# When a hybrid encoder layer fetches its parked residual, parked half embedding, norm weights and embedding input

## Chip, cores and metric

One NeuronCore of one Trainium2 chip runs the whole layer in one launch. The metric is device time in microseconds (us) of one execution. Before the change the median of three runs is 1164.94 us (1162.43 to 1167.7).

## What is computed

One layer on 256 tokens of width 2048, all float32. The part that matters here is the second half:

```
h  = h + rms_norm(mixed, g_mix_post)
fn = rms_norm(h, g_ffn_pre)
ff = (silu(fn @ w_ffn_gate) * (fn @ w_ffn_up)) @ w_ffn_down      # 2048 -> 5632 -> 2048
h  = h + rms_norm(ff, g_ffn_post)
gate = sigmoid(rms_norm(h, g_ple_pre) @ w_ple_gate)
ple  = p @ w_ple_proj                                            # 256 -> 2048
h  = h + rms_norm(gate * ple, g_ple_post)
```

## The kernel before

Every product is made of three fp32r matmuls: a float32 operand is split into a high and a low part, and high x high, high x low and low x high are summed in PSUM (lines 661 to 663). The weights stream through SBUF in tiles of 512 KB (256 rows x 512 columns): SyncE (SP) issues the load of a raw tile `wr` (line 522), ScalarE (ACT) casts it to the high part `wh` (line 614), VectorE (DVE) subtracts to get the low part `wl` (line 627), and TensorE (PE) uses both in 12 matmuls of 128x512. There are 4 buffers of `wr` and 4 pairs of `wh` and `wl`. A raw buffer is free once its `wl` is made; a pair is free once PE has used it. So the load of a tile waits for the `wl` of the tile four before it, and the cast of a tile waits for the last matmul of the tile four before it.

The feed-forward part runs over the 5632 columns in three parts (`PARTS`). In each part the gate and up products of its column blocks come first, then the down products of that part. The last part's down products take 24 weight tiles, called D1 to D24 here: D1 to D12 for output columns 0 to 1023, D13 to D24 for the rest. The last tile ahead of D1 is the last tile of `w_ffn_up`, called U here. The activations of the last block pass DVE (lines 1714 and 333), are moved between partitions by 16 small transfers `mT` (line 343; 8 issued by SP, 8 by POOL), are split on ACT and DVE (`mid2h`, `mid2l`, lines 305 and 307), and are used by D9 to D12 and D21 to D24.

Four things that are too large to keep, or are needed only later, are fetched again near the end:

- the residual `h`, parked in DRAM at line 1589 and fetched by `reload_h` (line 1596) in two transfers of 1024 KB. It is used at line 1535, after the last down product.
- the first half of the embedding `ple`, parked at line 1608 and fetched by `reload_half` (line 1614, 1024 KB). It is used when the gate of the embedding is applied (line 1856).
- the norm weights `g_ffn_post`, spread over all partitions by `next_gain` and `load_gain` (line 1422, 1024 KB). They are used at line 1478, when an output block of the down products is complete.
- the embedding input `pT`, fetched by `load_pT` (line 1410, tile `pw`, 256 KB) and split on ACT and DVE (lines 305 and 307, `pTh` and `pTl`). The products of `w_ple_proj`, after D24, use it.

The order of instructions on each engine is made at build time by a planner (`Plan`): every helper is a generator that yields the engine and the estimated cost of its next instruction, and the planner emits the instruction that could start first. A task gets two numbers: the time from which it is ready (`ready`), and a bonus (`late`, negative is earlier). The planner holds a transfer to be landed a fixed 2 us after its estimated duration (`LATENCY`). On the chip the order is fixed: each engine takes its instructions in that order, and an instruction whose data is not there holds up what stands behind it on its engine.

Of the kernel before, what the change touches and what calls it, by code (L numbers as in the profile page):

```python
# [18 lines left out]
NT = S // P  # L19
# [50 lines left out]
SOON = 2.0  # L70
# [6 lines left out]
class Event:  # L77


    t = None  # L80
# [141 lines left out]
def dve(n, take=None, give=None):  # L222
    return ("dve", COST["dve"] + 0.00104 * n, None, take, give)
# [6 lines left out]
def dma(kb, take=None):  # L230
    return ("dma", kb / 340.0, None, take, None)
# [3 lines left out]
def layer(ctx: ExitStack, tc: tile.TileContext, a: dict, out: bass.AP):  # L235
    nc = tc.nc
# [4 lines left out]
    plan = Plan(wr=R_BUFS, w=W_BUFS, sm=SM_BUFS, acc=4, ev=1, mid=2, bt=2, m2=1, mt=1, sq=1, T0=1, T1=1, T4=1, **{f"{s}{j}": n for s, m, n in (("p", 3, 1), ("t", 3, 0)) for j in range(m)}, wr0=1, w0=1)  # L241

    def f32(t):
        return t.bitcast(F32)
# [14 lines left out]
    def w_kind(i):  # L259
        return f"w{more_w[i]}" if i in more_w else "w"  # L260
# [15 lines left out]
    def raw_kind(i):  # L276
        if i in lower:
            return f"p{lower[i]}"
        return f"wr{more_raws[i]}" if i in more_raws else "wr"
# [22 lines left out]
    def split(hi, lo, src, n, give=None):  # L302

        yield act(n)
        nc.scalar.copy(hi, src)
        yield dve(n, give=give)
        nc.vector.tensor_tensor(out=lo, in0=src, in1=f32(hi), op=ALU.subtract)
# [57 lines left out]
    def done(event):  # L365
        event.t = plan.now
# [63 lines left out]
    class Group:  # L430
# [23 lines left out]
        def two(self, j):  # L454
            i = len(tiles)
            tiles.append(None)
            self.twos.append(i)
            lower[self.own[j] + 1] = j
            segs.append((two_products, self, j, i))
# [47 lines left out]
    def pieces(i):  # L507

        return [slice(0, 1), slice(1, 2)] if i < EARLY else [slice(0, 2)]
# [77 lines left out]
    def last_sum(i):  # L587
        late, last, j, js, _, _ = fours[i]
        b = (3, 6, 7)[j]
        there = Event()  # L590
        yield from added(blocks()[:, b, :], late[:, 0, :], there)
        yield there
        if j == js[-1]:
            raws[last] = blocks()[:, 3:7:3, :] if len(js) == 2 else blocks()[:, 7:8, :]
            done(ev_raw[last, 2])
# [21 lines left out]
    def lo_stream():  # L617
        last_one = max(f[1] for f in fours.values())
        for i in range(len(tiles)):
            at_lo[0] = i  # L620
            for j in pieces(i):
                n = j.stop - j.start
                yield ev_hi[i, j.stop]
                src = raws[i] if n == 2 else raws[i][:, j, :]
                m = slice(j.start, j.start + src.shape[1])
                yield dve(src.shape[1] * N, give=gives.get(i) or raw_kind(i) if j.stop == 2 else None)
                nc.vector.tensor_tensor(  # L627
                    out=los[i][:, m, :], in0=src, in1=f32(his[i][:, m, :]), op=ALU.subtract
                )
                done(ev_lo[i, j.stop])  # L630
            raws.pop(i)
            if i == half_end:
                plan.add(reload_half(), plan.now, -SOON)
            if i in fours:
                plan.add(last_sum(i), plan.now, -2 * SOON)
            if i == last_one:
                done(ev_ple)
# [31 lines left out]
    def product(dst, x, i, j, start=False, stop=False, seeded=False):  # L669
        plan.main(3 * MM)  # L670
        wh, wl = his[i][:, j, :], los[i][:, j, :]
        nc.tensor.matmul(dst, x[0], wh, start=start, stop=False, skip_group_check=seeded)  # L672
        nc.tensor.matmul(dst, x[1], wh, start=False, stop=False, skip_group_check=seeded)  # L673
        nc.tensor.matmul(dst, x[0], wl, start=False, stop=stop, skip_group_check=seeded)  # L674

    def spent(i):
        his.pop(i), los.pop(i)
        at_pe[0] = max(at_pe[0], i)
        free_w(i)
        plan.run()  # L680

    def block(lhs, kx, t):
        return [x[:, t * P : (t + 1) * P] for x in lhs.at[kx]]
# [49 lines left out]
    def two_products(group, j, i):  # L733
        (C1, _, _), (C2, _, _) = group.chunks
        kx = group.sevens[j][1]
        s = group.lhs.sums[kx]
        plan.main(0, ev_lo[i, 2], group.lhs.ev[kx + 1], group.made)
        product(C1.accs[0], block(group.lhs, kx + 1, 0), i, 0, seeded=True)
        product(C2.accs[0], s["S4"], i, 1, seeded=True)
        spent(i)  # L740
        if i == last_two:
            plan.add(reload_h(), plan.clk["pe"], -SOON)
        if i == last_third:
            plan.add(load_pT(), plan.clk["pe"], -SOON)

    def one_product(group, js, i):
        (C1, _, _), _ = group.chunks
# [39 lines left out]
    def free_w(i):  # L787
        if i not in keep:
            plan.free[w_kind(i)].append(plan.clk["pe"])
        if i == max(more_w):  # L790
            plan.add(next_gain(("ffn", "g_ffn_post"), plan.clk["pe"]), plan.clk["pe"])

    keep = set()
    def run_seg(s):
# [580 lines left out]
    t2 = {}  # L1375
# [27 lines left out]
    def pT_pair():  # L1403
        return [t2["pool"].tile([P, 2, S], F32R, tag=n, name=n) for n in ("pTh", "pTl")]

    def load_pT():
        yield dma(256, take="mt")
        here = Event()
        pw = t2["pool"].tile([P, 2, S], F32, tag="mt", name="pw")
        nc.sync.dma_start(pw, a["pT"].rearrange("(k p) s -> p k s", p=P))  # L1410
        done(here)
        yield here
        hi, lo = pT_pair()
        yield from split(hi, lo, pw, 2 * S, give="mt")
        pT[1].blocks(hi, lo, 0, 2)
        pT[1].pair(0)
    ev_gain = {}

    def load_gain(n):
        yield dma(1024)  # L1420
        g = t2["pool"].tile([P, D], F32, tag="gain", name=f"gain_{n}")
        nc.sync.dma_start(g, a[n].to_broadcast([P, D]))
        t2["gain"] = g
# [136 lines left out]
    def turn_h(c, hi, lo, nxt, gname):  # L1560
# [18 lines left out]
    spill = ctx.enter_context(  # L1579
        tc.tile_pool(name="spill", bufs=1, space=bass.MemoryType.DRAM)  # L1580
    ).tile([NT, P, D], F32, name="h_spill")
    ev_spilled, ev_back = Event(), Event()
# [6 lines left out]
            nc.sync.dma_start(spill[t], t2["h"].tiles[t])  # L1589
        done(ev_spilled)  # L1590

    def reload_h():
        t2["h"] = Halves(t2["pool"], "h")
        for t in range(NT):
            yield dma(1024)
            nc.sync.dma_start(t2["h"].tiles[t], spill[t])
        done(ev_back)

    half_spill = ctx.enter_context(
        tc.tile_pool(name="half_spill", bufs=1, space=bass.MemoryType.DRAM)  # L1600
# [11 lines left out]
    def reload_half():  # L1612
        yield dma(1024)
        nc.sync.dma_start(t2["ple"][:, :, 0 : D // 2], half_spill)
        done(ev_half_back)

    def next_gain(g, ready):
        yield from load_gain(g[1])
        done(ev_gain[g[0]])
# [63 lines left out]
    ffn = Sub("ffn", "g_ffn_post", "g_ple_pre")  # L1683
# [332 lines left out]
    for i, (_, last, _, js, _, two) in fours.items():  # L2016
        ev_load[i], ev_load[i + 1] = Event(), Event()
        gives[i], gives[i + 1], gives[two] = f"T{first_slot[i]}", raw_kind(i), raw_kind(i + 1)
        gives[last] = tuple(f"t{j}" for j in js)
    twos = [(j, i) for f, g, j, i in (s for s in segs if s[0] is two_products)]  # L2020
    last_two = max(i for _, i in twos)
    last_third = max(i for j, i in twos if j == 2)
# [22 lines left out]
    plan.add(hi_stream(), late=lambda: lateness(at_hi))  # L2045
    plan.add(sum_stream(), late=-LATE)
    plan.add(lo_stream(), late=lambda: lateness(at_lo))
    plan.add(make_hT(0), late=lambda: -2 * LATE if at_hi[0] else -LATE)
    plan.add(make_hT(1), late=lambda: -2 * LATE if at_hi[0] else -LATE)
# [96 lines left out]
```

## Time and profile before

| | |
|---|---|
| runs | 1162.43, 1164.94, 1167.7 us |
| profiled execution | 1163.89 us, span 1162.1 us |
| TensorE busy | 1148.7 us of the span, mean granted clock 0.997 |
| DVE, ACT busy | 883.0 us, 703.0 us |
| DMA | 257.21 MB, mean 221 GB/s |
| D1 starts, D24 ends | 990.1 us, 1055.4 us after the span's start |

A row of a timeline gives the start and the duration in us, the engine (a q marks the issue of a transfer by the engine's sequencer), the line, the operation, output <- inputs, the shape and the number of instructions merged into the row; in square brackets is how long the engine had been idle and who ended that. A row of transfers gives their number, the KB of one, and the median us from issue to landing. A row of stretches gives for each engine its busy time and its number of instructions, then the granted clock, the busy share of the DMA engines and their GB/s.

### The profile page before, as it was taken

Reading aid. Unit: us, or ns where it says so; the run is one execution under the profiler, and the core shown is the slowest. Engines: PE = TensorE matmul, PEld = TensorE weight load, DVE = VectorE, ACT = ScalarE, POOL = GpSimd, SP = SyncE. Lnnn points to the kernel's source line nnn. Section 1 sums busy time; section 2 is a strip of 40 time slices with the busy share of each in tenths; the row PEclk is TensorE's granted clock in tenths of the full one; section 3 lists DMA queues with packets and bytes.
Section 4 is the critical chain, followed back from the end, with each engine's and each line's share of the span. In section 5 each row is a group of like instructions: output and inputs, shape, how many; then the busy total and the mean of one; then the engine's idle time right before and its main releaser. Section 6 shows DMA issues by size and latency. Waiting matters only on the chain.

```text
span 1162.1 us, 15025 instructions
## 1 busy us (share of the span) xinstructions
PE 1148.7 (99%) x5225; PEld 951.3 (82%) x5225; DVE 883.0 (76%) x1096; ACT 703.0 (60%) x933; POOL 120.9 (10%) x198
## 2 busy tenths in 40 slices
PE   9999999999999999999999999999999999999997
PEld 7888888888888888788888888888888887887786
DVE  6678787888468777988778888887778884668575
ACT  6777777875456655655546556565455554456564
POOL 0000000000000123031000223312000311100000
PEclk9999999999999999999999999999999999999999
DMA  9867566546676887876775777877667668854772
GB/s 315 288 188 222 185 181 206 175 149 211 228 272 197 291 256 226 261 215 203 252 224 190 249 224 205 263 239 216 207 208 252 205 216 291 249 190 161 216 248 77
DMA packets 109964, 257.21 MB, mean 221 GB/s; under 512 B 38976, under 2 KB 46144, under 8 KB 108736
## 3 DMA queue, kind: packets, MB, share of 16 engines
q1 hardware_dynamic: 99552, 241.73, 62.5%
q0 software_dynamic: 9904, 14.17, 7.4%
q8 instruction: 41, 0.67, 0.2%
q10 hardware_dynamic: 432, 0.35, 0.1%
q14 instruction: 35, 0.29, 0.1%
HBM read 242.57 MB, written 5.24 MB: 213 GB/s over the span
## 4 chain that ended last, share of the span: by engine, by line
PE 86%; DMA 5%; DVE 4%; ACT 2%; issue 1%; POOL 1%; SPq 0%; ACTq 0%; DVEq 0%; POOLq 0%
PE acc L663 23%; PE acc L662 23%; PE acc L661 23%; PE acc L674 4%; PE acc L673 4%; PE acc L672 4%; DMA mT<-mid 3%; DVE wl L627 1%; POOL mT L343 1%; PE tr L324 1%; ACT wh L614 1%; DMA wr<-in_w_ple_gate 1%; DMA pw<-in_pT 1%; PE warm L2055 0%; PE pg L355 0%
## 5 line engine op out<-in xcount | busy, mean ns | idle before, releaser
L627 DVE TENSOR_TENSOR wl<-wr,wh 128x1024 fp32r<-128x1024 f32 (+1 forms) x313 | 373.9, 1209 | 131.7 <-ACT wh L614 129.7
L614 ACT CAST wh<-wr 128x1024 fp32r<-128x1024 f32 (+1 forms) x313 | 323.8, 1043 | 212.0 <-PE acc L662 142.0
L661 PE MATMUL acc<-wh,hT_mix_hi 128*128 128x512 f32 x420 | 164.4, 391 | 2.6 <-ACT wh L614 2.6
L662 PE MATMUL acc<-wh,hT_mix_lo 128*128 128x512 f32 x420 | 164.1, 391 | 0.3 <-DVE hT_mix_lo L313 0.3
L663 PE MATMUL acc<-wl,hT_mix_hi 128*128 128x512 f32 x420 | 164.2, 391 | 0.1
L343 POOL DMA_DIRECT2D mT<-mid x152 | 88.5, 589 | 570.0 <-DMA wr<-in_w_ffn_up 401.9
L663 PE MATMUL acc<-wl,hT_hi 128*128 128x512 f32 x320 | 124.9, 391 | 0.0
L661 PE MATMUL acc<-wh,hT_hi 128*128 128x512 f32 x316 | 124.4, 394 | 0.0
L662 PE MATMUL acc<-wh,hT_lo 128*128 128x512 f32 x316 | 123.1, 390 | 0.0
L661 PEld LDWEIGHTS acc<-wh,hT_mix_hi 128*128 128x128 f32 x420 | 79.2, 189 | 19.3 <-ACT wh L614 3.0
L614 ACT CAST wh<-ple 128x1024 fp32r<-128x1024 f32 (+1 forms) x52 | 51.8, 995 | 70.6 <-DVE ple L566 26.5
L663 PEld LDWEIGHTS acc<-wl,hT_mix_hi 128*128 128x128 f32 x420 | 79.1, 188 | 17.5 <-DVE wl L627 1.3
L662 PEld LDWEIGHTS acc<-wh,hT_mix_lo 128*128 128x128 f32 x420 | 79.2, 189 | 17.3 <-DVE hT_mix_lo L313 1.0
L663 PEld LDWEIGHTS acc<-wl,hT_hi 128*128 128x128 f32 x320 | 60.1, 188 | 13.6 <-DVE wl L627 0.9
L627 DVE TENSOR_TENSOR wl<-ple,wh 128x1024 fp32r<-128x1024 f32 (+1 forms) x52 | 59.6, 1150 | 13.7 <-ACT wh L614 13.1
L662 PEld LDWEIGHTS acc<-wh,hT_lo 128*128 128x128 f32 x316 | 59.4, 188 | 11.7
L661 PEld LDWEIGHTS acc<-wh,hT_hi 128*128 128x128 f32 x316 | 59.4, 188 | 11.3
L583 POOL DMA_DIRECT2D ple<-in_w_ffn_up x27 | 24.0, 887 | 245.1 <-DVE wl L627 164.7
L627 DVE TENSOR_TENSOR w<-wr,w 128x1024 fp32r<-128x1024 f32 x29 | 35.4, 1220 | 10.3 <-ACT w L614 9.7
L614 ACT CAST w<-wr 128x1024 fp32r<-128x1024 f32 x29 | 30.5, 1052 | 19.7 <-PE acc L662 14.5
L627 DVE TENSOR_TENSOR wl<-third,wh 128x1024 fp32r<-128x1024 f32 x29 | 35.4, 1221 | 8.6 <-ACT wh L614 7.7
L661 PE MATMUL acc<-wh,hT_ffn_hi 128*128 128x512 f32 x104 | 40.9, 393 | 0.6 <-ACT hT_ffn_hi L311 0.6
(429 smaller groups left out, 2389.9 us busy)
## 6 DMA issues: line engine op xcount, KB each, us to landing
wr<-in_w_in SPq DMA_DIRECT2D x77, 512.0 KB, 4.6
wr<-in_w_ffn_gate SPq DMA_DIRECT2D x70, 512.0 KB, 5.3
wr<-in_w_ffn_down SPq DMA_DIRECT2D x70, 512.0 KB, 4.7
wr<-in_w_ffn_up SPq DMA_DIRECT2D x55, 512.0 KB, 5.7
wr<-in_w_out SPq DMA_DIRECT2D x32, 512.0 KB, 4.0
wr<-in_w_ple_gate SPq DMA_DIRECT2D x32, 512.0 KB, 4.5
lower<-in_w_ffn_up SPq DMA_DIRECT2D x18, 512.0 KB, 5.0
third<-in_w_ffn_gate SPq DMA_DIRECT2D x18, 512.0 KB, 5.9
```

Source lines behind the costliest of these rows:

```text
L324: nc.tensor.transpose(tr[:, b, t * P : (t + 1) * P], e[:, t, sl], ident)
L343: (nc.gpsimd if i in pool else nc.sync).dma_start(dst[32 * j : 32 * j + 32, :, :, i, :], src[32 * i : 32 * i + 32, :, :, j, :],)
L583: nc.gpsimd.dma_start(dst, src, accum_op=ALU.add)
L614: nc.scalar.copy(his[i][:, 0 : src.shape[1], :] if n == 2 else his[i][:, j, :], src)
L627: nc.vector.tensor_tensor(out=los[i][:, m, :], in0=src, in1=f32(his[i][:, m, :]), op=ALU.subtract)
L661: nc.tensor.matmul(accs[t], hi[:, sl], his[i][:, j, :], start=st, stop=False, **group)
L662: nc.tensor.matmul(accs[t], lo[:, sl], his[i][:, j, :], start=False, stop=False, **group)
L663: nc.tensor.matmul(accs[t], hi[:, sl], los[i][:, j, :], start=False, stop=sp, **group)
L672: nc.tensor.matmul(dst, x[0], wh, start=start, stop=False, skip_group_check=seeded)
L673: nc.tensor.matmul(dst, x[1], wh, start=False, stop=False, skip_group_check=seeded)
L674: nc.tensor.matmul(dst, x[0], wl, start=False, stop=stop, skip_group_check=seeded)
```

## The change

The times from which the four fetches are ready are moved, and the two halves of the residual become two tasks of their own. The bonus that had put them ahead of the weight tiles is gone.

```diff
@@ lo_stream
             if i == half_end:
-                plan.add(reload_half(), plan.now, -SOON)
+                plan.add(reload_half(), plan.now + 64.0)
@@ two_products
         if i == last_two:
-            plan.add(reload_h(), plan.clk["pe"], -SOON)
+            for t in range(NT):
+                plan.add(reload_h(t), plan.clk["pe"] + 28.0 + 13.0 * t)
         if i == last_third:
-            plan.add(load_pT(), plan.clk["pe"], -SOON)
+            plan.add(load_pT(), plan.clk["pe"] + 22.0)
@@ free_w
         if i == max(more_w):
-            plan.add(next_gain(("ffn", "g_ffn_post"), plan.clk["pe"]), plan.clk["pe"])
+            plan.add(next_gain(("ffn", "g_ffn_post"), plan.clk["pe"] + 27.0), plan.clk["pe"] + 27.0)
@@ reload_h
-    def reload_h():
-        t2["h"] = Halves(t2["pool"], "h")
-        for t in range(NT):
-            yield dma(1024)
-            nc.sync.dma_start(t2["h"].tiles[t], spill[t])
-        done(ev_back)
+    halves_back = []
+
+    def reload_h(t):
+        if "back" not in t2:
+            t2["back"] = Halves(t2["pool"], "h")
+        yield dma(1024)
+        nc.sync.dma_start(t2["back"].tiles[t], spill[t])
+        halves_back.append(t)
+        if len(halves_back) == NT:
+            t2["h"] = t2["back"]
+            done(ev_back)
```

On SP, the queue of transfers from the last two gate and up tiles to the end of the down tiles was this before the change (the rows of `w_ffn_down` are D1 to D24 in order):

```order
L1614 DMA ple<-ple_spill 128x2x1024
L1422 DMA gain_g_ffn_post<-in_g_ffn_post 128x2048
L1596 DMA h_8087<-h_spill 128x2048
L522 DMA wr<-in_w_ffn_gate 128x1024
L522 DMA wr<-in_w_ffn_up 128x1024
L522 DMA wr<-in_w_ffn_down 128x1024
L1596 DMA h_8088<-h_spill 128x2048
L522 DMA wr<-in_w_ffn_down 128x1024
L1410 DMA pw<-in_pT 128x2x256
L522 DMA wr<-in_w_ffn_down 128x1024 x4
L343 DMA mT<-mid 32x8x32 x8
L522 DMA wr<-in_w_ffn_down 128x1024 x18
```

The same stretch of SP's queue with the change:

```order
L522 DMA wr<-in_w_ffn_gate 128x1024
L522 DMA wr<-in_w_ffn_up 128x1024
L522 DMA wr<-in_w_ffn_down 128x1024 x6
L343 DMA mT<-mid 32x8x32 x8
L522 DMA wr<-in_w_ffn_down 128x1024 x4
L1423 DMA gain_g_ffn_post<-in_g_ffn_post 128x2048
L1599 DMA h_8084<-h_spill 128x2048
L1411 DMA pw<-in_pT 128x2x256
L522 DMA wr<-in_w_ffn_down 128x1024 x4
L1599 DMA h_8085<-h_spill 128x2048
L522 DMA wr<-in_w_ffn_down 128x1024 x6
L1620 DMA ple<-ple_spill 128x2x1024
```

All five fetches have moved behind U. The norm weights, the first half of the residual and the embedding input now stand in a row between D10 and D11, the second half of the residual between D14 and D15, and the half embedding between D20 and D21.

On ACT, the casts before the change around the split of the embedding input (the one cast ahead of `pTh` is that of the last gate tile, the three behind it are those of U, D1 and D2):

```order
L305 CAST mid2h_7734<-mT 128x512 x2
L614 CAST wh<-wr 128x1024
L305 CAST pTh<-pw 128x512
L614 CAST wh<-wr 128x1024 x3
L1695 ACTIVATE mid<-acc_7774,rstd_f 128x512
L1695 ACTIVATE mid<-acc_7775,rstd_f 128x512
L614 CAST wh<-wr 128x1024 x4
L305 CAST mid2h_8304<-mT 128x512 x2
L614 CAST wh<-wr 128x1024 x9
L1496 ACTIVATE junk,ss_ffn<-mg 128x512 x2
```

The same stretch of ACT with the change:

```order
L305 CAST mid2h_7734<-mT 128x512 x2
L614 CAST wh<-wr 128x1024 x4
L1701 ACTIVATE mid<-acc_7774,rstd_f 128x512
L1701 ACTIVATE mid<-acc_7775,rstd_f 128x512
L614 CAST wh<-wr 128x1024 x4
L305 CAST mid2h_8293<-mT 128x512 x2
L614 CAST wh<-wr 128x1024 x3
L305 CAST pTh<-pw 128x512
L614 CAST wh<-wr 128x1024 x6
L1497 ACTIVATE junk,ss_ffn<-mg 128x512 x2
```

The split of the embedding input has moved from ahead of the cast of U to between the casts of D9 and D10. On DVE its second half (`pTl`) has moved in the same way, from ahead of the `wl` of U to between the `wl` of D9 and D10. Nothing else changes its place on ACT or DVE, and PE and POOL keep their order.

## Prediction

> **What bounds the kernel now.** The page comes first. It says which engine sets the time:
>
> ```profile
> span 1162.1 us, 15025 instructions
> PE 1148.7 (99%) x5225; PEld 951.3 (82%) x5225; DVE 883.0 (76%) x1096; ACT 703.0 (60%) x933; POOL 120.9 (10%) x198
> ```
>
> PE is busy for 99% of the span, so the kernel gets faster only where PE stands still or runs slowly. The fetches that move stood between 960 and 976 us, and the next view is the list of waits from 980 us to the end (who waited for whom, total, times, longest):
>
> ```profile
> ACT pTh L305 <- DMA pw<-in_pT: 5.9, 1, 5.9
> PE acc L661 <- ACT wh L614: 2.6, 1, 2.6
> ```
>
> ACT waited 5.9 us for the embedding input, and PE waited 2.6 us for a cast of ACT, each once. The timelines of PE and of ACT show that the two belong together:
>
> ```profile
> 982.56 0.39 PE L663 MATMUL acc<-wl,hT_mix_hi 128*128 128x512 f32 x1
> 985.53 0.80 PE L661 MATMUL acc<-wh,hT_mix_hi 128*128 128x512 f32 x1 [2.59 <-ACT wh L614]
> ...
> 990.13 0.39 PE L661 MATMUL acc<-wh,mid2h 128*128 128x512 f32 x1
> ```
>
> ```profile
> 977.00 1.05 ACT L614 CAST wh<-wr 128x1024 fp32r<-128x1024 f32 x1 [3.06 <-DMA wr<-in_w_ffn_gate]
> 983.92 0.62 ACT L305 CAST pTh<-pw 128x512 fp32r<-128x512 f32 x1 [5.87 <-DMA pw<-in_pT]
> 984.44 2.93 ACT L614 CAST wh<-wr 128x1024 fp32r<-128x1024 f32 x3
> ```
>
> The split `pTh`, which nothing needs before D24 is done, stood in ACT's queue ahead of the cast of U. Its data came at 983.9, so the cast of U began at 984.44, and PE's first matmul with U at 985.53 instead of 0.227 us after 982.56. It did not resume at full speed either. The stretches show why (columns: PE, PEld, DVE, ACT, POOL, granted clock, DMA share, GB/s):
>
> ```profile
> 984.00:986.00 2.00, 0.47 (x1) 0.47 (x2) 1.18 (x2) 2.00 (x3) 0.00 (x0) 0.86 0.05 20
> 986.00:988.00 2.00, 1.96 (x5) 1.06 (x5) 2.00 (x3) 2.00 (x4) 0.00 (x0) 0.50 0.18 31
> ```
>
> The granted clock fell to 0.50 behind the pause. So the price of the wait is read from start to start. D15 and D1 stand 14 tiles apart, and D10 is between them:
>
> ```profile
> 1014.61 0.39 PE L661 MATMUL acc<-wh,mid2h 128*128 128x512 f32 x1
> ...
> 1028.21 0.39 PE L661 MATMUL acc<-wh,mid2h 128*128 128x512 f32 x1
> ```
>
> (1028.21 - 990.13) / 14 = 2.72 us for one weight tile without a pause, 0.227 us for a matmul. U would have begun at 982.56 + 0.23 = 982.79 and D1 at 985.51. D1 began at 990.13, so the wait cost **4.62 us**: 2.74 of standing still, 1.88 at the low clock.
>
> **Step 1: the wait at U goes.** Why was `pw` late? SP's timeline, and behind it the transfers with their time to landing:
>
> ```profile
> 959.98 0.60 SPq L1614 DMA_DIRECT2D ple<-ple_spill  x1
> 963.26 0.33 SPq L1422 DMA_DIRECT2D gain_g_ffn_post<-in_g_ffn_post  x1
> 963.64 1.09 SPq L1596 DMA_DIRECT2D h<-h_spill  x1
> 968.09 0.33 SPq L522 DMA_DIRECT2D wr<-in_w_ffn_gate  x1
> 969.46 0.33 SPq L522 DMA_DIRECT2D wr<-in_w_ffn_up  x1
> ```
>
> ```profile
> ple<-ple_spill SPq DMA_DIRECT2D x1, 1024.0 KB, 9.8
> gain_g_ffn_post<-in_g_ffn_post SPq DMA_DIRECT2D x1, 1024.0 KB, 9.9
> h<-h_spill SPq DMA_DIRECT2D x1, 1024.0 KB, 12.0
> wr<-in_w_ffn_gate SPq DMA_DIRECT2D x1, 512.0 KB, 8.8
> pw<-in_pT SPq DMA_DIRECT2D x1, 256.0 KB, 7.9
> ```
>
> Landings follow the order of issue: 969.8, 973.2, 975.6 for the three of 1024 KB, 976.9 for the last gate tile. With the five fetches out of the way, the gate tile and U are issued at the same 968.09 and 969.46, since these times are set by `wl` of earlier tiles. They land after 3.4 to 4.6 us, the fastest and the median of this row of tile `wr` from 955 to 1060 us:
>
> ```profile
> DMA to landing us min/median/max: 3.4/4.6/8.8
> ```
>
> That is 974.1 at the latest for U. Its cast then needs only a free pair, which PE gives back when the tile four before U ends, at 982.79 - 3 x 2.72 = 974.6. What would be late next? Even with 8.8 us, U would be there at 978.3 and ready by 980.6, before 982.79, so no other wait stands close behind the removed one. Nothing is added or removed in work: the same transfers, casts and subtractions run, and one more task is none on the chip. Gain: 4.62 us, and everything behind moves up by that.
>
> **Step 2: `pTh` waits again, now ahead of the cast of D10.** By the order on SP, `pw` stands behind D7 to D10, the norm weights and one half of `h`. D7 is issued when the eight `mT` are, and these wait for a transpose on DVE that hangs on the end of U:
>
> ```profile
> 992.46 5.70 SPq L343 DMA_DIRECT2D mT<-mid  x8
> 998.26 38.36 SPq L522 DMA_DIRECT2D wr<-in_w_ffn_down  x18
> ```
>
> ```profile
> 1002.42 1.05 ACT L614 CAST wh<-wr 128x1024 fp32r<-128x1024 f32 x1 [0.60 <-DMA wr<-in_w_ffn_down]
> ...
> 1004.94 1.06 ACT L614 CAST wh<-wr 128x1024 fp32r<-128x1024 f32 x1 [0.21 <-DMA wr<-in_w_ffn_down]
> 1006.42 1.06 ACT L614 CAST wh<-wr 128x1024 fp32r<-128x1024 f32 x1 [0.42 <-PE acc L662]
> ```
>
> These casts are of D7, D9 and D10. D7 and D9 waited for their landing, at 1002.4 and 1004.9: 1.26 us for 512 KB. 4.62 us earlier D9 lands at 1000.3 and D10 at 1001.6. The norm weights, `h` and `pw` are 2304 KB, 4.5 times 512 KB, so 5.7 us: `pw` lands at 1007.3. The cast of D10 follows 0.52 us later at 1007.8. In the old rows `wl` of D10 began 1.09 us after its cast and took 1.22:
>
> ```profile
> 1007.51 1.22 DVE L627 TENSOR_TENSOR wl<-wr,wh 128x1024 fp32r<-128x1024 f32 x1 [0.26 <-ACT wh L614]
> ```
>
> so it is done at 1010.1. PE reaches D10 at 1014.61 - 4.62 = 1009.99 and needs `wl` at its third matmul, 0.45 us later, at 1010.44. The margin is 0.3 us, where it was 6.3. I take **0 us** here. Bounds: below, 0, since PE cannot gain at a place where it did not wait; above, the two transfers of 1024 KB landed 3.4 and 2.4 us behind their forerunners in the crowd at 960 us, which adds 0.7 to the three and makes the loss 0.4; at the 2.3 us that the rival below takes, it is 2.0.
>
> The Trainium skill (HBM Reference, "Specifications (TRN2)") gives about 358 GB/s as the effective rate of one core and calls more than that the case of a core that streams alone. By 358 GB/s, as an estimate from that page, the three transfers take 6.6 us and step 2 costs 0.6 us; the 1.26 us of this trace are 416 GB/s, and they decide.
>
> **Step 3: D15 comes later.** The load of D14 is issued when `wl` of D10 is done, at 1010.1 and no longer at 1008.76 - 4.62 = 1004.1. The second half of `h` stands behind D14, and D15 behind that. D14 lands 3.4 us (fastest) to 4.6 us (median) later, at 1013.5 to 1014.7; `h` adds 2.5, D15 1.3, so D15 lands at 1017.3 to 1018.5. Its old cast and what stands behind it on DVE:
>
> ```profile
> 1020.02 1.05 ACT L614 CAST wh<-wr 128x1024 fp32r<-128x1024 f32 x1 [1.67 <-PE acc L662]
> 1020.98 0.62 ACT L1496 ACTIVATE junk<-mg 128x512 f32<-128x512 f32 x1
> ```
>
> ```profile
> 1021.73 1.31 DVE L1478 TENSOR_TENSOR mg<-mg,gain_g_ffn_post 128x512 f32<-128x512 f32 x2 [0.79 <-ACT junk L1496]
> ...
> 1024.49 1.31 DVE L1478 TENSOR_TENSOR mg<-mg,gain_g_ffn_post 128x512 f32<-128x512 f32 x2 [0.26 <-ACT junk L1496]
> 1025.71 3.49 DVE L627 TENSOR_TENSOR wl<-wr,wh 128x1024 fp32r<-128x1024 f32 x3
> ```
>
> The squares (`junk`) wait behind the cast of D15, the products with the norm weights wait for the squares, and `wl` of D15 waits for those: one chain without slack. `wl` of D15 ended at 1025.71 + 1.22 = 1026.9, PE needed it at 1028.21 + 0.45: 1.7 us of margin. The cast moves from 1015.4 (the old one less 4.62) to 1017.3 or 1018.5, 1.9 to 3.1 us later, so PE waits 0.2 to 1.4 us. I take **0.5 us**, nearer to the fast landing because the queue is already running when D14 joins it.
>
> **What costs nothing.** The norm weights land at about 1004 and are used from about 1018. The second half of `h` is there by 1018 and needed after D24, about 1051. The half embedding puts 2.5 us ahead of D21. The load of D21 is issued when `wl` of D17 is made, which PE needs by 985.51 + 16 x 2.72 + 0.45 = 1029.5; from then the two take at most 2.5 + 4.6 us, the cast and `wl` 2.3, so D21 is ready at 1038.9, and PE needs it at 1040.4. If that cover went, each microsecond would be one of PE. The `mT` of the block before, which POOL issued while the five fetches ran, only get faster.
>
> **The sum.** 4.62 - 0 - 0.5 = 4.1 us off the profiled execution, 1163.89 to 1159.8 us. That execution lies 1.05 us under the median of the three runs; off the median the forecast is 1164.94 - 4.1 = **1160.8 us**.
>
> **Rivals.** *(a) The wait moves instead of going.* If `pw` lands later than 1007.6, ACT holds up D10 as it held up U, and each further microsecond is one of PE. For it: the same instruction, again ahead of a cast that PE needs soon, with 4096 KB in front of its transfer from D7 on. Against: the 1.26 us of the rows. If the three take 8 us instead of 5.7, D10 costs 2.0 and the end is 1162.8 on the median. At a pause of 2.7 us or more the clock may fall as at U, and all of the gain is gone: 1164.9 or a little above. The other pause that bears on this is shorter, and the clock stayed at 1.00 behind it:
>
> ```profile
> 469.65 0.50 PE L674 MATMUL acc<-wl,hT_mix_hi 128*128 128x512 f32 x1 [1.10 <-DVE wl L627]
> ...
> 470.00:472.00 2.00, 2.00 (x10) 1.66 (x9) 2.00 (x3) 2.00 (x3) 0.00 (x0) 1.00 0.80 167
> ```
>
> So a pause of 1.1 us costs itself alone, one of 2.6 costs 1.9 more, and the change lies between. The Trainium skill (TensorE: Matmul & The Clock Gate, "What's actually happening") puts the fall behind an idle window of about 3.4 us; by that rule a second pause of 2.7 us would cost itself alone and rival (a) would still end 1.9 us ahead. The pause of 2.59 us with the clock of 0.50 behind it speaks against the rule as a threshold.
>
> *(b) The queue becomes the bound: slower.* From D7 on, 18 tiles and 4352 KB more must land before D24 is cast, 13.9 MB between 993.6 and about 1046. That needs 284 GB/s; at 259 GB/s the delay has eaten the 4.62 us, and below that the kernel is slower. At the mean of this line, 221 GB/s, they would take 63 us, 13.9 too long, and the end would be 1174:
>
> ```profile
> DMA packets 109964, 257.21 MB, mean 221 GB/s; under 512 B 38976, under 2 KB 46144, under 8 KB 108736
> ```
>
> Against it: that mean is of a queue that mostly waits for free buffers, and the tiles that stood in line took 1.26 us each.
>
> *(c) More than the wait goes.* If an ordinary execution loses more at U than the profiled one, since the landing of `pw` differs from run to run, a further 1.5 to 2 us may be had: 1159 or less.
>
> **How the numbers follow.** Forecast with step 3 between 0 and 1.4: 0.60. (a): 0.26. (b): 0.06. (c): 0.08. The range takes in the forecast with nothing given back, 1160.3, less the 2.5 us by which the lowest run lies under the median, and (a) with all given back, 1164.9, plus 2: 1157.8 to 1167. A change of 0.5%, 5.8 us, is about what a measurement of this kernel can tell from no change. The forecast lies 1.7 us short of it and the runs scatter by more than that, so a part of its chance (0.2 of 0.6) and most of (c) go to faster: 0.27. (b) and the end of (a) give slower 0.07. Within 0.5%: 0.66.
>
> **What would show it.** After: ACT's row for `pTh` no longer stands ahead of U, PE goes from the last gate tile through U to D1 without a gap, and the clock is 1.00 from 984 to 990: step 1. The time from D1 to D24 and the idle time at D10 (step 2, `pTh` waiting for `pw`, landing at about 1007.3) and at D15 (step 3, `wl`) give the rest. I am wrong if PE stops at D10 for over a microsecond, if ACT waits for tiles of `w_ffn_down` again and again after D11, or if a gap remains at U, which would mean that something else than `pw` held it.

## The result, and the profile after

Ten runs of the changed kernel have a median of 1161.2 us (1159.38 to 1162.69), ten of the kernel before 1164.6 us (1161.61 to 1167.7). The ratio is 0.9968, 95% interval 0.9956 to 0.9979: 3.7 us less, 2.4 to 5.1. The forecast was 1160.8 us and "within 0.5%".

The profiled execution took 1159.38 us, span 1157.6. That is 4.5 us less than the profiled one of before, but the two spans can't be set against each other for the change: PE starts the tile two ahead of U at 975.69 here and at 977.35 before. This difference of 1.66 us arose earlier: PE's order up to that tile is the same, and in both executions the 400 matmuls ahead of it take 90.67 us, without a pause. So the stretch from that tile to the first product with `pTh` is compared: 27 tiles, which take 27 x 2.72 = 73.44 us without a pause. PE's timeline of before and then of after gives its ends:

```profile
977.35 0.39 PE L661 MATMUL acc<-wh,hT_mix_hi 128*128 128x512 f32 x1
...
1055.41 0.39 PE L661 MATMUL acc<-wh,pTh 128*128 128x512 f32 x1
```

```profile
975.69 0.39 PE L661 MATMUL acc<-wh,hT_mix_hi 128*128 128x512 f32 x1
...
981.13 0.39 PE L661 MATMUL acc<-wh,hT_mix_hi 128*128 128x512 f32 x1
...
983.85 0.39 PE L661 MATMUL acc<-wh,mid2h 128*128 128x512 f32 x1
...
1008.10 0.39 PE L663 MATMUL acc<-wl,mid2h 128*128 128x512 f32 x1
...
1009.82 0.50 PE L663 MATMUL acc<-wl,mid2h 128*128 128x512 f32 x1 [0.53 <-DVE wl L627]
...
1023.33 0.39 PE L662 MATMUL acc<-wh,mid2l 128*128 128x512 f32 x1
1024.28 0.50 PE L663 MATMUL acc<-wl,mid2h 128*128 128x512 f32 x1 [0.57 <-DVE wl L627]
...
1051.16 0.39 PE L661 MATMUL acc<-wh,pTh 128*128 128x512 f32 x1
```

Before: 78.06 us, 4.62 lost. After: 75.47, 2.03 lost. The pause at U is gone: U begins at 981.13 and D1 one tile of 2.72 us later. Two new ones stand where the prediction looked for them. Over D10 (the last matmul of D9 starts at 1008.10) PE loses 1.17 us, start to start, over what the matmuls need, and over D15 (its second matmul starts at 1023.33) 0.86. The granted clock stays at 1.00, here around U and around D10:

```profile
982.00:984.00 2.00, 2.00 (x10) 1.65 (x10) 0.56 (x1) 1.14 (x3) 0.00 (x0) 1.00 0.64 229
1008.00:1010.00 2.00, 1.41 (x6) 0.55 (x5) 1.74 (x3) 1.92 (x3) 0.00 (x0) 1.00 0.39 152
```

ACT shows where the wait went: it stands 5.87 us for `pw`, as long as in the kernel before, now ahead of the cast of D10 (the first of the three at 1007.46). Behind D12 it waits for the landing of D13, D14 and D15 in turn:

```profile
1006.93 0.62 ACT L305 CAST pTh<-pw 128x512 fp32r<-128x512 f32 x1 [5.87 <-DMA pw<-in_pT]
1007.46 3.12 ACT L614 CAST wh<-wr 128x1024 fp32r<-128x1024 f32 x3
1010.77 1.06 ACT L614 CAST wh<-wr 128x1024 fp32r<-128x1024 f32 x1 [0.19 <-DMA wr<-in_w_ffn_down]
1013.54 1.05 ACT L614 CAST wh<-wr 128x1024 fp32r<-128x1024 f32 x1 [1.71 <-DMA wr<-in_w_ffn_down]
1017.33 1.05 ACT L614 CAST wh<-wr 128x1024 fp32r<-128x1024 f32 x1 [2.73 <-DMA wr<-in_w_ffn_down]
```

On SP, D7 to D10, the norm weights, `h` and `pw` go out in a row:

```profile
991.75 1.77 SPq L522 DMA_DIRECT2D wr<-in_w_ffn_down  x4
993.61 0.61 SPq L1423 DMA_DIRECT2D gain_g_ffn_post<-in_g_ffn_post  x1
994.28 0.68 SPq L1599 DMA_DIRECT2D h<-h_spill  x1
997.59 0.38 SPq L1411 DMA_DIRECT2D pw<-in_pT  x1
```

And their time to landing: D7 5.4 us, D10 (issued at 993.14) 8.0, the norm weights 10.1, `h` 11.9, `pw` 9.3:

```profile
wr<-in_w_ffn_down SPq DMA_DIRECT2D x1, 512.0 KB, 5.4
wr<-in_w_ffn_down SPq DMA_DIRECT2D x1, 512.0 KB, 8.0
gain_g_ffn_post<-in_g_ffn_post SPq DMA_DIRECT2D x1, 1024.0 KB, 10.1
h<-h_spill SPq DMA_DIRECT2D x1, 1024.0 KB, 11.9
pw<-in_pT SPq DMA_DIRECT2D x1, 256.0 KB, 9.3
```

### The profile page after: what moved, and what is told of

Read it like the earlier page. It is cut to its first block, busy times and chain, and to the rows that moved or that the text cites. A ratio compares the mean times of both kernels' runs of the same rounds, so it can differ in the third digit from the quotient of the medians.

```text
span 1157.6 us, 15025 instructions
## 1 busy us (share of the span) xinstructions
PE 1146.8 (99%) x5225; PEld 950.5 (82%) x5225; DVE 882.6 (76%) x1096; ACT 703.6 (61%) x933; POOL 120.8 (10%) x198
## 4 chain that ended last, share of the span: by engine, by line
PE 88%; DMA 4%; DVE 3%; ACT 1%; issue 1%; POOL 1%; SPq 1%; ACTq 0%; DVEq 0%; POOLq 0%
PE acc L662 24%; PE acc L663 24%; PE acc L661 24%; PE acc L674 4%; PE acc L673 4%; PE acc L672 4%; DMA mT<-mid 2%; DMA wr<-in_w_ffn_down 1%; PE tr L324 1%; DVE wl L627 1%; DMA pw<-in_pT 1%; POOL mT L343 1%; ACT wh L614 0%; SPq L343 0%; PE warm L2061 0%
## 5 line engine op out<-in xcount | busy, mean ns | idle before, releaser
L662 PEld LDWEIGHTS acc<-wh,hT_mix_lo 128*128 128x128 f32 x420 | 78.8, 188 | 17.3 <-DVE hT_mix_lo L313 1.0
L662 PE MATMUL acc<-wh,hT_ffn_lo 128*128 128x512 f32 x104 | 40.8, 393 | 0.5 <-DVE hT_ffn_lo L313 0.5
```

The lines of the kernel that those rows point to most:

```text
L662: nc.tensor.matmul(accs[t], lo[:, sl], his[i][:, j, :], start=False, stop=False, **group)
```

## The experiments

The theory is that of the prediction: the pause at U, and the one at D10, come from one instruction, `pTh`, standing in ACT's strict order ahead of a cast that PE needs, while its transfer stands in line; D15 is late because `h` stands ahead of it. The rival is that the amount of transfer in a stretch is what counts: the crowd ahead of U before, the three in a row behind D10 after. For each kernel the table gives what PE loses in the 27 tiles of its profiled execution, and its runs against runs of the kernel before on the same chip.

| kernel | lost in the stretch, us | where | median, us | ratio to before, 95% interval |
|---|---|---|---|---|
| before | 4.62 | U | 1164.6 | |
| changed | 2.03 | D10 1.17, D15 0.86 | 1161.2 | 0.9968 (0.9956 to 0.9979) |
| 1: before, split of `pT` later | 0.00 | | 1159.58 | 0.9964 (0.9952 to 0.9977) |
| 2: changed, `pT` at its old time | 0.00 | | 1159.18 | 0.9959 (0.9943 to 0.9975) |
| 3: changed, split of `pT` later | 0.54 | D15 | 1159.77 | 0.9959 (0.9944 to 0.9974) |
| 4: changed, 1024 KB more ahead of `pT` | 4.94 | D10 | 1163.73 | 0.9998 (0.9988 to 1.0008) |
| 5: before, `pT` alone at its new time | 0.12 | D8 | 1160.16 | 0.9958 (0.9944 to 0.9973) |
| 6: changed, `h` behind D17 | 0.79 | D10 | 1159.06 | 0.9958 (0.9945 to 0.9971) |
| 7: changed, 512 KB more ahead of `pT` | 4.21 | D10 | 1163.82 | 0.9993 (0.9983 to 1.0003) |

### 1. The kernel before, with only the split moved

```diff
@@ load_pT
         done(here)
-        yield here
+        plan.add(split_pT(pw), plan.now + 6.0)
+
+    def split_pT(pw):
         hi, lo = pT_pair()
         yield from split(hi, lo, pw, 2 * S, give="mt")
```

> The kernel before with one thing moved: the split of the embedding input stands behind the casts of U, D1 and D2 on ScalarE (and behind their low parts on VectorE) instead of ahead of them; every transfer keeps its place in the queue. Theory (the pause at U is only the order on ScalarE): no pause at U, none at D10 or D15, 4.6 us off, about 1160.0 against 1164.6 of before. Rival (the crowd of transfers holds U or D1 up anyway): a pause stays at U or D1, gain under 1.5 us, 1163 or more.

Measured: 1159.58 us, nothing lost. ACT's timeline shows the crowd still there (the casts of the last gate tile, U and D1 wait for their landings), but the casts go on as tiles land, and the split follows when `pw` is there:

```profile
977.80 1.05 ACT L614 CAST wh<-wr 128x1024 fp32r<-128x1024 f32 x1 [2.49 <-DMA wr<-in_w_ffn_gate]
979.09 1.06 ACT L614 CAST wh<-wr 128x1024 fp32r<-128x1024 f32 x1 [0.24 <-DMA wr<-in_w_ffn_up]
980.36 1.06 ACT L614 CAST wh<-wr 128x1024 fp32r<-128x1024 f32 x1 [0.21 <-DMA wr<-in_w_ffn_down]
...
986.29 0.62 ACT L305 CAST pTh<-pw 128x512 fp32r<-128x512 f32 x1
```

PE's stretch has no gap at all (PE busy 73.40 of 73.40, clock 1.00):

```profile
978.40:1051.80 73.40, 73.40 (x325) 60.81 (x324) 47.15 (x48) 37.96 (x49) 4.61 (x8) 1.00 0.71 229
```

Not one transfer had to be moved to get the whole 4.62 us. This decides step 1 for the order on ACT and against the crowd by itself.

### 2. The changed kernel, with the embedding input at its old time

```diff
         if i == last_third:
-            plan.add(load_pT(), plan.clk["pe"] + 22.0)
+            plan.add(load_pT(), plan.clk["pe"], -SOON)
```

> The changed kernel, but the embedding input is fetched and split at its old time, ahead of the cast of U; the other four fetches stay where the change put them. Theory: without the crowd in front its transfer lands about 4 us after its issue, near 974, U has several us to spare, so no pause at U; nothing stands ahead of D10, so its load chain is early and D15 has no pause either: 4.6 us off before, about 1160.0, and 1.2 to 2 us below the changed kernel. Rival (the split ahead of U costs PE whatever stands in front of its transfer): a pause of 1 us or more at U, 1161 or more.

Measured: 1159.18 us, nothing lost, neither at U nor at D10 or D15. `pTh` stands ahead of U as before and still holds ACT up, by 4.78 us, but it is done at 979.8 and not at 984.5:

```profile
979.14 0.62 ACT L305 CAST pTh<-pw 128x512 fp32r<-128x512 f32 x1 [4.78 <-DMA pw<-in_pT]
```

The theory had the transfer landing near 974. It was issued only at 974.99, and landed 4.1 us later: on SP it stands behind D2, issued at 974.36, and its buffer is that of `mT`, whose last reader ended at 974.90. The margin at U was large enough for that: PE reaches U at 984.2. So a wait on ACT costs nothing where PE has tiles in hand until the wait is over. Together with experiment 1 this says that the pause at U needed both, the split ahead of the cast and the crowd ahead of `pw`.

### 3. The changed kernel, with only the split moved

The edit is that of the first experiment, with 24.0 in place of 6.0.

> The changed kernel with the split of the embedding input moved from ahead of the cast of D10 to behind that of D18; all transfers keep their place in the queue. Theory: the 1.1 us lost at D10 go, D14 is asked for earlier, so at D15 0 to 0.4 us are lost instead of 0.8: 1.5 to 2 us below the changed kernel, about 1159.5. Rival (the three fetches in a row make the queue the bound from D10 on): ScalarE waits for the tiles of D11 to D15 instead, PE loses about as much as with the change, 1161 or more.

Measured: 1159.77 us; D10 loses nothing, D15 0.54. The queue is as full as with the change, and ACT does wait for the landings: the cast of D11, landed at 1010.23, begins at 1010.33, and then ACT waits for D12, D13 and D14 in turn, 0.2 us each. PE does not wait for any of these (the rows are the casts of D13, D14 and D15):

```profile
1012.83 1.05 ACT L614 CAST wh<-wr 128x1024 fp32r<-128x1024 f32 x1 [0.19 <-DMA wr<-in_w_ffn_down]
1014.10 1.05 ACT L614 CAST wh<-wr 128x1024 fp32r<-128x1024 f32 x1 [0.22 <-DMA wr<-in_w_ffn_down]
1017.80 1.05 ACT L614 CAST wh<-wr 128x1024 fp32r<-128x1024 f32 x1 [2.65 <-DMA wr<-in_w_ffn_down]
```

The loss at D10 was the order on ACT. D15 (the last row) is late without it too, a little more than expected (0.54 for 0 to 0.4), and here it is the queue that makes it late: from D10, landed at 1003.15, to D15, landed at 1017.71, one transfer lands right behind the other, 5888 KB in 14.56 us, which is 414 GB/s.

### 4. More ahead of the embedding input in the queue

```diff
         if i == last_two:
-            for t in range(NT):
-                plan.add(reload_h(t), plan.clk["pe"] + 28.0 + 13.0 * t)
+            plan.add(reload_h(0), plan.clk["pe"] + 28.0)
...
         here = Event()
+        for _ in reload_h(1):
+            pass
         pw = t2["pool"].tile([P, 2, S], F32, tag="mt", name="pw")
```

> The changed kernel with the second half of the residual (1024 KB) ahead of the embedding input in the queue instead of behind D14; same bytes, same order on all other engines. Theory: the embedding input lands 2.5 us later, ScalarE holds the cast of D10 by as much more, PE pauses 3.5 us at D10 and the clock falls to 0.5 behind it as it did at U, 1.7 to 1.9 us more; no loss at D15, since nothing stands behind D14: 5.2 to 5.6 lost at D10, 3.2 to 3.6 us above the changed kernel, about 1164.6. Without the fall of the clock: 1.5 to 1.9 above, about 1163. Rival (only the bytes in the stretch count, not what waits behind which): as the changed kernel, 1161.2.

Measured: 1163.73 us, 2.5 above the changed kernel, and 4.94 us lost, all at D10. ACT waits 8.32 us, PE pauses 2.76 us (start to start less one matmul), and the clock falls:

```profile
1011.48 0.62 ACT L305 CAST pTh<-pw 128x512 fp32r<-128x512 f32 x1 [8.32 <-DMA pw<-in_pT]
```

```profile
1013.10 0.50 PE L661 MATMUL acc<-wh,mid2h 128*128 128x512 f32 x1 [2.60 <-ACT wh L614]
...
1014.36 0.79 PE L663 MATMUL acc<-wl,mid2h 128*128 128x512 f32 x1 [0.43 <-DVE wl L627]
```

```profile
1014.00:1016.00 2.00, 1.64 (x4) 1.35 (x5) 1.99 (x3) 1.60 (x3) 0.00 (x0) 0.50 0.37 78
```

The bytes are the same, so the rival's 1161.2 is out. The loss is a little under the 5.2 to 5.6 expected, because the low clock cost less than the 1.7 to 1.9 taken for it. D1 begins at 985.86 here, so the third matmul of D10, the first that needs `wl`, was due at 985.86 + 9 x 2.72 + 0.45 = 1010.79. It came at 1014.36, 3.57 us late, and waited for `wl`; ACT and DVE set that time, not the clock. The other 4.94 - 3.57 = 1.37 us were lost behind it, at the low clock. This is the prediction's rival (a) at its end: the whole gain is gone.

### 5. The embedding input alone at its new time

The kernel before with the one line of `load_pT` taken from the change.

> The kernel before with the embedding input alone moved to its new time; the norm weights, the residual and the half embedding are fetched in the old crowd ahead of U. On SyncE the embedding input then stands directly behind D10, on ScalarE its split between the casts of D7 and D8. Theory: no pause at U although the crowd is still there (4.6 us back); the transfer lands one short transfer behind D10, so the cast of D8 waits about 3 us and PE loses 0 to 1.2 us at D8; no loss at D15: 3.4 to 4.6 us below before, 1159.7 to 1160.9. Rival (it takes the other three moves as well): a pause stays at U, 1163 or more.

Measured: 1160.16 us, 0.12 lost. The old crowd ahead of U stays and costs nothing. The split now waits 3.67 us ahead of the cast of D8, and PE gets through D8 with 0.1 us of delay:

```profile
1001.38 0.62 ACT L305 CAST pTh<-pw 128x512 fp32r<-128x512 f32 x1 [3.67 <-DMA pw<-in_pT]
```

So of the four fetches that the change moves, one line holds the whole gain, and by the traces the other three give 1.9 us of it back (2.03 - 0.12).

### 6. The second half of the residual further behind

```diff
-                plan.add(reload_h(t), plan.clk["pe"] + 28.0 + 13.0 * t)
+                plan.add(reload_h(t), plan.clk["pe"] + 28.0 + 18.0 * t)
```

> The changed kernel with the second half of the residual behind D17 in the queue instead of behind D14; nothing else moves. Theory: D15 lands 2.5 us earlier, so the 0.86 us lost at D15 go; the 1.17 us lost at D10 stay: 0.9 below the changed kernel, about 1160.3. Rival (D15 is late only because the load of D14 was asked for late behind D10): D15 still loses 0.5 us or more, 1161.

Measured: 1159.06 us. D15 loses nothing, D10 0.79:

```profile
1011.24 0.50 PE L663 MATMUL acc<-wl,mid2h 128*128 128x512 f32 x1 [0.47 <-DVE wl L627]
```

`h` ahead of D15 was the cause there, not the late request of D14 alone, which this kernel keeps. Up to D10 the order is that of the changed kernel, and yet 0.79 instead of 1.17 are lost: D10 landed 16.9 us after D1 began, there 17.3. So far two executions of the same order differ.

### 7. Half as much more ahead of it

As experiment 4, with columns 0 to 1023 of the second half of `h` ahead of `pw` and the rest in the changed kernel's place behind D14.

> The changed kernel with 512 KB of the second half of the residual ahead of the embedding input and 512 KB behind D14. Theory: the embedding input lands 1.26 us later than with the change, PE loses 1.26 more at D10 for that, 2.4 in all, and nothing at D15, since D14 is asked for later by what the smaller transfer saves and PE comes later too. If the clock falls behind a pause of 2 us, 1.5 to 1.9 more. So 1161.6 without the fall, 1163.3 with it. Rival (only the bytes in the stretch count): 1161.2 and the same losses as with the change.

Measured: 1163.82 us, 4.21 lost, all at D10. The pause is 2.45 - 0.23 = 2.22 us, and the clock falls:

```profile
1011.82 0.39 PE L663 MATMUL acc<-wl,mid2h 128*128 128x512 f32 x1
1014.27 0.76 PE L661 MATMUL acc<-wh,mid2h 128*128 128x512 f32 x1 [2.06 <-ACT wh L614]
...
1015.53 0.79 PE L663 MATMUL acc<-wl,mid2h 128*128 128x512 f32 x1
```

```profile
1014.00:1016.00 2.00, 1.65 (x3) 0.94 (x4) 1.75 (x2) 1.94 (x3) 0.00 (x0) 0.59 0.16 64
1016.00:1018.00 2.00, 2.00 (x6) 1.54 (x6) 2.00 (x3) 1.32 (x2) 0.00 (x0) 0.56 0.71 162
1015.00:1016.00 1.00, 0.92 (x3) 0.47 (x2) 1.00 (x2) 0.94 (x2) 0.00 (x0) 0.50 0.07 29
```

512 KB ahead of `pw` turned 2.03 us of loss into 4.21. They took 1.85 us to land behind the first half of `h` (1010.03 to 1011.88), not the 1.26 expected, and `pw` landed 25.1 us after D1 began, in the changed kernel 23.1. DVE's row shows when the `wl` of D10 was made:

```profile
1014.25 1.23 DVE L627 TENSOR_TENSOR wl<-wr,wh 128x1024 fp32r<-128x1024 f32 x1 [0.25 <-ACT wh L614]
```

The third matmul of D10 followed it at 1015.53. With D1 at 987.57 it was due at 1012.50, so 3.03 of the 4.21 us are the wait for `wh` and `wl`, and 1.18 came behind it at the low clock. In the changed kernel the same matmul was 1.04 late. So the later landing is the larger part of the difference (2.0 us), the low clock the smaller (about 1.0), and the 0.86 at D15 went.

The medians of experiments 1, 2, 3, 5 and 6 lie 1.0 to 2.1 us under the changed kernel's, but their intervals overlap with its own and with each other. That they beat the changed kernel is shown by the pauses in one trace of each, not by the runs, and which of them is the best is not shown; that they beat the kernel before is shown by both.

## Why the prediction was right, point by point

- **Step 1, the wait at U goes: right, in mechanism and size.** The 4.62 us are gone from the trace, and experiment 1 gets them by the order on ACT alone, experiment 2 by the transfers alone. "No other wait stands close behind the removed one" held even with the old crowd (experiments 1 and 5).
- **Step 2, `pTh` ahead of the cast of D10: the mechanism was right, the size was not.** 0 us were taken, with 0.4 as the upper bound short of rival (a); 1.17 were lost. The prediction had named a stop of over a microsecond at D10, and waits of ACT for tile after tile behind D11, as signs that it is wrong, and both are there, though the waits for D13 and D14 cost PE nothing. The mis-sized term is the landing of D7. It was taken from the row of before, 4.1 us after its issue; it took 5.4. Counted from D1, D10 landed at 1001.18 - 983.85 = 17.3 us instead of 16.1, and `pw` at 23.1 instead of 21.8. The rest of the sum held: D10 to `pw` took 5.73 us for 5.7 predicted, 412 GB/s. By the 358 GB/s of the Trainium skill (HBM Reference, "Specifications (TRN2)") they would have taken an estimated 6.6; the trace speaks for the higher rate. With a margin of 0.3 us, 1.3 us more had to show; the margin was too thin to forecast 0.
- **Step 3, D15 comes later: right, a little larger.** 0.86 for 0.5 taken, within 0.2 to 1.4. D14 was asked for 1.3 us later than predicted, by what `pw` was late, and PE came 1.17 later too. Experiment 6 shows that the place of `h` decides it.
- **What costs nothing: right.** D21 and the later tiles show no pause, and the norm weights and the residual were there in time.
- **The sum.** 4.1 us were forecast; the stretch gives 2.59 in one execution, the medians 3.4, the ratio 2.4 to 5.1. That the forecast lies only 0.4 us from the median is in part luck. By the profiled executions the errors of steps 2 and 3 make 1.17 + 0.36 = 1.5 us; the median of before came out 0.34 lower with ten runs than with three, and the rest lies within the scatter of the runs, of which the loss at D10 is a part (1.17 and 0.79 with one order).
- **Rival (a)** is what part of the change became, at 1.17 us; its far end, all gain lost, is real and 512 to 1024 KB away (experiments 7 and 4). The prediction left open where between 1.1 and 2.6 us of pause the clock falls: 2.22 was enough in experiment 7. But the 1.88 us that the prediction puts down to the low clock at U are not all the clock's. DVE made the `wl` of U only behind its late cast, and the third matmul of U waited for it (kernel before, DVE and PE):

```profile
985.51 1.23 DVE L627 TENSOR_TENSOR wl<-wr,wh 128x1024 fp32r<-128x1024 f32 x1 [0.26 <-ACT wh L614]
```

```profile
986.79 0.80 PE L663 MATMUL acc<-wl,hT_mix_hi 128*128 128x512 f32 x1
```

That matmul was due at 982.79 + 0.45 = 983.24 and came 3.55 us late, right behind the end of `wl` at 986.74; at a full clock it would have waited for `wl` as long. The low clock took the remaining 4.62 - 3.55 = 1.07 us, as it took 1.37 and 1.18 in experiments 4 and 7.
- **Rival (b)**, the queue as the bound, is out for the stretch as a whole and real at one place: with the same transfers experiment 3 loses 0.54 us at D15, at the end of a line that moves 414 GB/s, and nothing behind it. The rate that the prediction names for it is a little high: 13.9 MB between 993.6 and 1046 need 265 GB/s, not 284.
- **Rival (c)** was not seen.

## What to carry to other kernels

Ask of a prefetch not only when its data is needed but where its first consumer stands: an instruction in strict order that waits for a transfer holds up all that is behind it on its engine, and moving the transfer moves the wait along unless the consumer is moved past the landing. Then count the time in hand of the tile behind the consumer: waits of 5.87, 5.87 and 4.78 us cost 4.62 us (before), 1.17 (changed) and nothing (experiment 2). Count the whole chain up to the first matmul that cannot run, here the cast and the low part, ahead of any price for the clock: in the three kernels whose clock fell, that chain cost 3.0 to 3.6 us and the low clock 1.1 to 1.4 more.

## What the runs showed of the hardware that was not expected

- **The clock.** Pauses of 2.22, 2.74 and 2.76 us (experiment 7, before, experiment 4) were each followed by a granted clock of 0.50. If the clock was either 1.00 or 0.50, the two stretches of 2 us shown for experiment 7 give (1 - 0.59) x 2 / 0.5 + (1 - 0.56) x 2 / 0.5 = 3.4 us at half speed. Pauses of 0.72 us at D15 and of 1.1 us (before, at 469.65) were not followed by it. Where between 1.1 and 2.22 us the limit lies, and whether there is a fixed one, no run here shows. The Trainium skill (TensorE: Matmul & The Clock Gate, "What's actually happening") speaks of an idle window of about 3.4 us; the duration of the slow phase agrees with that window, the pause that is enough for it is shorter here.
- **Landing behind small transfers.** D7 is issued right behind the sixteen `mT`. In the kernel before and experiments 1, 2 and 5 it landed 3.9 to 4.2 us after its issue, in the changed kernel and experiments 3, 4, 6 and 7 5.2 to 5.7. What sets the two groups apart was not found. Experiment 2 has the norm weights and `h` queued behind D10 before D7 lands, as the changed kernel has, and is fast; but they are asked for 0.9 and 0.7 us later after D7 than there. This is the term that step 2 missed, and its cause stays open.
